# Stick-breaking attention: softplus' high parts on ScalarE, weights' sums behind the value products, head 0's scores inside the values' projection, another order at the end

## The chip, the cores and the metric

The kernel runs on one core of one Trainium2 chip. The metric is the device time of one execution in microseconds (us); of several runs the median counts.

## The reference, cut to what matters

The whole program is two transformer blocks of width 1024 over 512 tokens. The change touches one part of the second block, the stick-breaking attention with 16 heads of 64:

```python
qkv = (h @ w_qkv).reshape(b, s, 3, SB_HEADS, HEAD_DIM)
...
z = jnp.einsum('bqhd,bshd->bhqs', q_blk, k) * scale
log_1m = jnp.where(causal, jax.nn.log_sigmoid(-z), 0.0)      # minus softplus(z)
excl = lax.cumsum(log_1m, axis=3, reverse=True) - log_1m     # sum over later keys
a = jnp.where(causal, jnp.exp(jax.nn.log_sigmoid(z) + excl), 0.0)
o = jnp.einsum('bhqs,bshd->bqhd', a, v)
...
return o.reshape(b, s, SB_HEADS * HEAD_DIM) @ w_o
```

So each head needs its scores z, softplus(z), the running sum of softplus over the keys between a key and the query, the exponential of z less those sums, and the product with the values. An output projection follows over all heads.

## The kernel before, in words

Every engine works off its own queue in the order in which the code issues. There is no scheduler behind it: the order is written out by hand.

Products in full precision are built from two rounded parts of each operand, a high and a low one: three matmuls (high x high, low x high, high x low) for one. A weight matrix comes in pieces of 128 x 1024. `Weights` loads a piece by DMA on SP's queue (`ws`, L327), ScalarE rounds it to the high part (`wh`, L340), and VectorE subtracts to get the low part (`wl`, L349). `W.get` of one piece issues these two steps for the piece two further on. A projection of one piece is 24 matmuls (`group`, or `tokens` for the values).

The attention is `s_all`. Its steps:

- The values of the first eight heads are projected (`values(0)`: four weight pieces `sv0.0` to `sv0.3`, 96 matmuls into four banks of PSUM), then the norm's sums, then the projections of queries and keys of head pair 0, then the values of the other eight heads (`values(1)`). ScalarE moves the values out of PSUM. The residual is multiplied by its gain on VectorE in eight tiles (L1520, three buffers `back`) and spilled to DRAM by eight DMAs on SP's queue.
- A loop of 18 rounds follows (`for i in range(16 + last)`). In round i the table `S_ORDER` is walked: each entry names a step and its lag, so ("low", 1) in round i is the low part of head i - 1. The steps: `proj`, a projection of queries or keys of a later pair, always into the single bank `bp`; `scores` (PE, into the banks `za` and `zb`, two of each); `low` (VectorE, L1688); `evac`, the projection out of its bank (VectorE, L1611); `cap` (VectorE, two operations, L1659 and L1660); `qparts` and `kparts`, the high and low parts of queries or keys (ScalarE, VectorE, for keys two DMAs on SP's queue as well); `exp` (ScalarE, an exponential and a logarithm, L1665 and L1666); `soft`, the maximum with the scores (VectorE, L1672 and L1673); `high` (GpSimd, three operations, L1681 to L1683: a copy of 128 columns, an addition of 128 columns, the rounded copy of all 1280 columns); `weights` (PE, the sums over later keys, added to the scores in their banks: matmuls with the high parts and with the low parts of softplus); `a` (ScalarE, exponential out of the two banks, L1713 and L1714); `out` (PE, the value product, for two heads at a time in odd rounds) and `join` (ScalarE, the result out of its bank into `h`, L1733).
- While the last heads run, the output projection begins. `S_LEAD` says after which step of which round the pieces of `start(n)` are issued: products `out(m, ks)` of output tile m with the head pairs ks. `S_SPLIT` says where the pairs' results are split into high and low parts (`split(p)`: a rounded copy on ScalarE, L547, and a subtraction on VectorE, L548). Behind the loop the rest of the output projection is issued, and its results are added to the spilled residual.

Tiles with few buffers set further bounds: the high and low parts of softplus have one buffer each (`sp=1`), the capped scores two (`sT=2`).

Of the kernel before, what the change touches and what calls it, by code (L numbers as in the profile page):

```python
# [13 lines left out]
AF = mybir.ActivationFunctionType  # L14
ALU = mybir.AluOpType
# [450 lines left out]
class Kernel:  # L466
# [992 lines left out]
    def _stick(self):  # L1459
# [14 lines left out]
        for j, scale in enumerate((-NEG, 0.0, -NEG)):  # L1474
# [3 lines left out]


    S_ORDER = (("proj", 0), ("scores", 0), ("low", 1), ("evac", 0), ("cap", 0),  # L1480
               ("qparts", 0), ("kparts", 0), ("exp", 0), ("soft", 0), ("high", 0),
               ("weights", 1), ("a", 1), ("out", 2), ("join", 2))
    S_BUFS = dict(sT=2, sA=4, sp=1, st=2, back=3)
    S_LEAD = ((14, "proj"), (14, "join"), (15, "cap"), (15, "out"), (17, "kparts"))
    S_SPLIT = ((14, "cap"), (14, "scores"), (14, "out"), (14, "kparts"), (14, "out"),
               (14, "kparts"), (16, "a"))

    def s_all(self, norm, xh, xl):
        nc = self.nc
        self.turns = deque(["bp", "bo"])  # L1490

        def values(n):
            a, b, _ = self.zbanks()
            a2 = self.bank("za")
            pss = [a, a2, b[:, 0], b[:, 1]]
            for kk in range(4):
                self.tokens(pss, self.W.get(f"sv{n}.{kk}"), xh, xl, kk)
            for c, ps in enumerate(pss):
                nc.scalar.activation(self.vf[:, c, 8 * n:8 * n + 8, :],
                                     ps.rearrange("p (h d) -> p h d", h=8), AF.Copy,  # L1500
                                     scale=norm.tm[:, c:c + 1] if n else 1.0)

        values(0)
        norm.ssq()
        qk, rest = {}, []
        _, b, _ = self.zbanks(False)
        for kind in range(2):
            rest.append(self.sproj(kind, 0, xh, xl, norm, qk, b[:, kind]))
# [8 lines left out]
        for k in range(KT):  # L1517
            if isinstance(norm, Norm2):
                t = self.tmp("back", bufs=self.S_BUFS["back"])
                nc.vector.scalar_tensor_tensor(t, self.h[:, k, :], gf[:, k:k + 1],  # L1520
                                               norm.bc1, op0=ALU.mult, op1=ALU.mult)
            else:
                t = self.h[:, k, :]
            nc.sync.dma_start(out=self.dram[:, k, :], in_=t)
        self.hd, self.zs = {}, {}
        ox = None
        lead = []

        def out(m, ks):
            w, ps = lead[m]  # L1530
            self.group(ps, w, *ox, ks, 0 in ks, 7 in ks)

        def split(p):
            self.split(ox[0][:, p, :], ox[1][:, p, :], self.h[:, p, :])

        ws = []

        def start(n):

            nonlocal ox  # L1540
            if n == 0:
                ox = self.newx()
                lead.append((self.W.get("so0", 1), self.bank("bp")))
            elif n == 1:
                out(0, range(2))
            elif n == 2:
                ws.extend(self.W.get(f"so{m}", 0) for m in (1, 2))
                out(0, range(2, 6))
            elif n == 3:
                _, b, _ = self.zbanks(False)  # L1550
                for j in range(2):
                    lead.append((ws[j], b[:, j]))
                out(1, range(6))
            elif n == 4:
                ws.append(self.W.get("so3", 0))
                out(2, range(6))
                for m in range(3):
                    out(m, [6])

        last = max(lag for _, lag in self.S_ORDER)  # L1560
        self.qk, self.pend = qk, {}
        for i in range(16 + last):
            for part, lag in self.S_ORDER:
                u = i - lag
                if part == "proj":
                    if u < 14:
                        self.pend[u] = self.sproj(u % 2, u // 2 + 1, xh, xl, norm, qk)
                elif part in ("evac", "qparts", "kparts"):
                    if 0 <= u < 14 and part != ("kparts", "qparts")[u % 2]:
                        self.pend[u] = self.pend[u]()  # L1570
                elif 0 <= u < 16:
                    getattr(self, "s_" + part)(u)
                for n, (at, p) in enumerate(self.S_LEAD):
                    if (i, part) == (at, p):
                        start(n)
                for n, (at, p) in enumerate(self.S_SPLIT):
                    if (i, part) == (at, p):
                        split(n)
        split(7)
        lead.append((ws[2], self.bank("za")))  # L1580
        out(3, range(4))
        nxt, nx = self.next_norm() if self.nxt else None, self.newx() if self.nxt else None
        self.back, self.fetched, self.back_tag = {}, 0, ("back", self.S_BUFS["back"])
        self.fetch(2)
# [91 lines left out]
    def s_high(self, i):  # L1676

        t, za, zb = self.hd[i]
        s3 = self.tmp("sp3", (P, P), bufs=2)
        hi, lo = (self.tmp("sp" + a, (P, 1280), F32R, bufs=self.S_BUFS["sp"]) for a in "hl")  # L1680
        self.nc.gpsimd.tensor_scalar(s3, t[:, 1152:], 1.0, 0.0, op0=ALU.mult, op1=ALU.add)  # L1681
        self.nc.gpsimd.tensor_tensor(t[:, 1152:], t[:, 1152:], t[:, 1024:1152], op=ALU.add)
        self.nc.gpsimd.tensor_scalar(hi, t, 1.0, 0.0, op0=ALU.mult, op1=ALU.add)  # L1683
        self.hd[i] = [t, s3, hi, lo, za, zb]

    def s_low(self, i):
# [530 lines left out]
```

## Time and profile before

| | us |
|---|---|
| three runs | 2213.94, 2212.48, 2205.34 |
| median | 2212.48 |
| profiled execution | 2205.24 |
| its span | 2203.5 |

The profile is one execution, taken by the hardware profiler. Its page gives the busy time of each engine: PE is TensorE, DVE is VectorE, ACT is ScalarE, POOL is GpSimd, SP is the engine whose queue issues most DMAs. Other views list who waited for whom, the busy time in chosen stretches with the granted TensorE clock (1.00 is full), and the instructions of one engine in order of time. In these a row begins with its start, counted from the span's start, and its duration; an "x3" is three like instructions merged, and brackets hold the engine's idle time before it and what ended it. The attention lies between about 858 and 1135 us.

### The profile page before, as it was taken

The page shows a single profiled execution, that of the slowest core. Times are in us where ns is not written, and L with a number is a line of the kernel's source. Part 1 is how long each engine was busy: PE and PEld are TensorE (multiplying, and loading weights), DVE is VectorE, ACT ScalarE, POOL GpSimd, SP SyncE. Part 2 cuts the span into 40 slices and gives each one's busy share as a digit, 9 for nine tenths or more (in the row PEclk, how much of TensorE's full clock was granted, in tenths as well). Part 3 has the DMA queues.
Part 4 walks back from the last instruction along what each step waited for, and adds up shares of the span by engine and source line. Part 5 has one row for each costly group of instructions (what it writes and reads, how often), then busy time and mean ns, then how long its engine had stood idle before and what let it go on. Part 6 is the DMA issues. An engine that isn't in the chain of part 4 may idle for free.

```text
span 2203.5 us, 26617 instructions
## 1 busy us (share of the span) xinstructions
PE 2130.0 (97%) x10250; PEld 1730.3 (79%) x10250; DVE 1231.0 (56%) x2032; ACT 876.1 (40%) x1405; POOL 261.2 (12%) x324
## 2 busy tenths in 40 slices
PE   8899999999999999999999999999988899999998
PEld 6687888888888888777688888888766668888886
DVE  6988756554443435567655343446668755534334
ACT  4424434343222224355534232334547644423322
POOL 1333100000000000122200000001037730000000
PEclk9999999999999999999999999999999999999999
DMA  4222444123333323322143333334431123333331
GB/s 147 63 72 77 134 122 152 57 72 96 97 97 101 98 84 108 124 77 67 48 124 97 104 95 97 96 96 127 129 98 26 26 60 103 109 101 97 96 97 66
DMA packets 63375, 205.93 MB, mean 93 GB/s; under 512 B 7952, under 2 KB 8336, under 8 KB 63120
## 3 DMA queue, kind: packets, MB, share of 16 engines
q1 hardware_dynamic: 59504, 196.86, 30.1%
q10 hardware_dynamic: 3744, 7.37, 1.0%
q8 instruction: 80, 1.31, 0.2%
q14 instruction: 47, 0.39, 0.1%
HBM read 189.39 MB, written 6.29 MB: 89 GB/s over the span
## 4 chain that ended last, share of the span: by engine, by line
PE 78%; DVE 10%; ACT 4%; POOL 4%; issue 3%; DMA 1%; SPq 0%; ACTq 0%; POOLq 0%; DVEq 0%
PE psum L538 62%; PE b L538 14%; POOL sph L1683 1%; DVE wl L349 1%; ACT sT L1665 1%; ACT sT L1666 1%; DVE t L906 1%; PE psum L2090 1%; DVE spl L1688 1%; DVE sT L1660 1%; DVE np L2068 1%; DMA nq<-nq 1%; DVE pv L1087 0%; DVE sT L1659 0%; POOL np L2082 0%
## 5 line engine op out<-in xcount | busy, mean ns | idle before, releaser
L538 PE MATMUL psum<-xh,wh 128*128 128x512 f32 x1560 | 609.9, 391 | 1.5 <-DVE h L626 0.9
L538 PE MATMUL psum<-xh,wl 128*128 128x512 f32 x1560 | 607.5, 389 | 1.6 <-DVE wl L349 1.5
L538 PE MATMUL psum<-xl,wh 128*128 128x512 f32 x1560 | 607.2, 389 | 0.0
L340 ACT ACTIVATE wh<-ws 128x1024 fp32r<-128x1024 f32 (+1 forms) x346 | 356.5, 1039 | 371.7 <-PE psum L538 315.0
L349 DVE TENSOR_TENSOR wl<-ws,wh 128x1024 fp32r<-128x1024 f32 (+2 forms) x339 | 411.4, 1219 | 98.6 <-ACT wh L340 98.4
L538 PEld LDWEIGHTS psum<-xh,wl 128*128 128x128 f32 x1560 | 292.3, 187 | 64.8 <-DVE wl L349 2.9
L538 PEld LDWEIGHTS psum<-xh,wh 128*128 128x128 f32 x1560 | 292.4, 187 | 63.2 <-issue 2.3
L538 PEld LDWEIGHTS psum<-xl,wh 128*128 128x128 f32 x1560 | 292.4, 187 | 60.5
L538 PE MATMUL b<-xh,wh 128*128 128x512 f32 (+1 forms) x488 | 194.4, 398 | 6.6 <-ACT wh L340 6.6
L538 PE MATMUL b<-xh,wl 128*128 128x512 f32 (+1 forms) x488 | 191.9, 393 | 2.2 <-POOL wl L349 1.9
L538 PE MATMUL b<-xl,wh 128*128 128x512 f32 (+1 forms) x488 | 191.6, 393 | 0.0
L538 PE MATMUL psum<-hh,wh 128*128 128x512 f32 x320 | 125.0, 391 | 0.0
L538 PE MATMUL psum<-hh,wl 128*128 128x512 f32 x320 | 124.5, 389 | 0.0
L538 PE MATMUL psum<-hl,wh 128*128 128x512 f32 x320 | 124.5, 389 | 0.0
L1354 DVE TENSOR_TENSOR h<-h,psum 128x512 f32<-128x512 f32 x48 | 33.1, 689 | 161.2 <-PE psum L538 161.2
L1345 ACT ACTIVATE t<-t 128x512 f32<-128x512 f32 x64 | 40.5, 633 | 187.9 <-DVE t L1344 187.9
L538 PEld LDWEIGHTS b<-xh,wh 128*128 128x128 f32 (+1 forms) x488 | 92.0, 188 | 26.3 <-ACT wh L340 7.0
L538 PEld LDWEIGHTS b<-xh,wl 128*128 128x128 f32 (+1 forms) x488 | 91.5, 188 | 24.6 <-POOL wl L349 2.4
L538 PEld LDWEIGHTS b<-xl,wh 128*128 128x128 f32 (+1 forms) x488 | 92.1, 189 | 19.8 <-DVE xl L551 0.8
L1344 DVE SCALAR_TENSOR_TENSOR t<-psum,r_mlp 128x512 f32<-128x512 f32 x64 | 44.2, 690 | 79.1 <-PE psum L538 79.0
L538 PE MATMUL psum<-ks,nq 128*128 128x256 f32 (+2 forms) x256 | 72.6, 376 | 16.3 <-DVE nmx L2068 9.4
L2082 POOL TENSOR_SCALAR np<-np,nsm,gates 128x512 f32<-128x512 f32 (+3 forms) x128 | 81.8, 644 | 39.2 <-PE psum L2090 20.5
(488 smaller groups left out, 2947.1 us busy)
## 6 DMA issues: line engine op xcount, KB each, us to landing
ws<-in_wst SPq DMA_DIRECT2D x332, 512.0 KB, 3.5
h<-in_xT SPq DMA_DIRECT2D x16, 256.0 KB, 3.6
kk<-kk SPq DMA_DIRECT2D x16, 256.0 KB, 3.6
nq<-nq SPq DMA_DIRECT2D x16, 256.0 KB, 2.9
ws<-in_wst SPq DMA_DIRECT2D x8, 384.0 KB, 3.1
spill<-back SPq DMA_DIRECT2D x8, 256.0 KB, 2.0
back<-spill ACTq DMA_DIRECT2D x8, 256.0 KB, 3.6
spill<-h ACTq DMA_DIRECT2D x8, 256.0 KB, 5.7
```

The costliest lines, as they stand in the source:

```text
L340: self.nc.scalar.activation(hi[:, :n], s, AF.Copy)
L349: e.tensor_tensor(lo[:, :n], s, hi[:, :n].bitcast(F32), op=ALU.subtract)
L538: self.nc.tensor.matmul(ps, a, b, start=start, stop=stop, skip_group_check=again)
L906: nc.vector.scalar_tensor_tensor(t, u[:, q:q + T], cw[:, q:q + 1], t, op0=ALU.mult, op1=ALU.add)
L1344: nc.vector.scalar_tensor_tensor(t, ps, 0.0, norm.bc, op0=ALU.max, op1=ALU.mult)
L1345: nc.scalar.activation(t, t, AF.Square)
L1354: nc.vector.tensor_tensor(self.h[:, m, :], self.h[:, m, :], ps, op=ALU.add)
L1660: self.nc.vector.tensor_scalar(tb, zb[:, :, :384], 30.0, None, op0=ALU.min)
L1665: self.nc.scalar.activation(t, t, AF.Exp)
L1666: self.nc.scalar.activation(t, t, AF.Ln, bias=1.0)
L1683: self.nc.gpsimd.tensor_scalar(hi, t, 1.0, 0.0, op0=ALU.mult, op1=ALU.add)
L2082: self.nc.gpsimd.tensor_scalar(u["p"], u["p"], u.pop("sm"), self.gates[:, u["c"], e:e + 1], op0=ALU.mult, op1=ALU.mult)
```

## The change

Four edits in the attention:

- `s_high`: the rounded copy of softplus is divided. ScalarE copies columns 0 to 1151, GpSimd the last 128. GpSimd's other two operations stay.
- `S_ORDER`: `out` of head i - 2 is issued ahead of `weights` of head i - 1 instead of behind it, and `high` of head i behind `a` of head i - 1 instead of ahead of `weights`.
- `values(n)`: the banks are `bp`, `bo` and a `zb` pair. In `values(1)`, ahead of its third weight piece, the steps `scores`, `cap`, `exp`, `soft` and `high` of head 0 are issued; the loop leaves them out for head 0.
- The end: `S_LEAD` and `S_SPLIT` have other places. Splits begin in round 13, and their rounded copy is on GpSimd (`hi_pool=True`); the slabs that they fill are taken at the first split. Output tile 0 is issued in two parts of three pairs in round 14, tile 1 in round 15, tiles 2 and 3 in round 16; `out(3, range(4))`, which stood behind the loop and the last split, is now in round 16 ahead of the last value product.

```diff
@@ -1478,31 +1478,35 @@
 
 
     S_ORDER = (("proj", 0), ("scores", 0), ("low", 1), ("evac", 0), ("cap", 0),
-               ("qparts", 0), ("kparts", 0), ("exp", 0), ("soft", 0), ("high", 0),
-               ("weights", 1), ("a", 1), ("out", 2), ("join", 2))
+               ("qparts", 0), ("kparts", 0), ("exp", 0), ("soft", 0),
+               ("out", 2), ("weights", 1), ("a", 1), ("high", 0), ("join", 2))
     S_BUFS = dict(sT=2, sA=4, sp=1, st=2, back=3)
-    S_LEAD = ((14, "proj"), (14, "join"), (15, "cap"), (15, "out"), (17, "kparts"))
-    S_SPLIT = ((14, "cap"), (14, "scores"), (14, "out"), (14, "kparts"), (14, "out"),
-               (14, "kparts"), (16, "a"))
+    S_LEAD = ((14, "proj"), (14, "weights"), (15, "cap"), (15, "a"), (16, "out"), (16, "a"))
+    S_SPLIT = ((13, "a"), (13, "join"), (13, "join"), (14, "cap"), (14, "cap"), (14, "soft"),
+               (15, "join"))
 
     def s_all(self, norm, xh, xl):
         nc = self.nc
         self.turns = deque(["bp", "bo"])
 
         def values(n):
-            a, b, _ = self.zbanks()
-            a2 = self.bank("za")
-            pss = [a, a2, b[:, 0], b[:, 1]]
+            _, b, _ = self.zbanks(False)
+            pss = [self.bank("bp"), self.bank("bo"), b[:, 0], b[:, 1]]
             for kk in range(4):
+                if n and kk == 2:
+                    for part in ("scores", "cap", "exp", "soft", "high"):
+                        getattr(self, "s_" + part)(0)
                 self.tokens(pss, self.W.get(f"sv{n}.{kk}"), xh, xl, kk)
             for c, ps in enumerate(pss):
                 nc.scalar.activation(self.vf[:, c, 8 * n:8 * n + 8, :],
                                      ps.rearrange("p (h d) -> p h d", h=8), AF.Copy,
                                      scale=norm.tm[:, c:c + 1] if n else 1.0)
 
+        self.hd, self.zs = {}, {}
         values(0)
         norm.ssq()
         qk, rest = {}, []
+        self.qk = qk
         _, b, _ = self.zbanks(False)
         for kind in range(2):
             rest.append(self.sproj(kind, 0, xh, xl, norm, qk, b[:, kind]))
@@ -1522,7 +1526,6 @@
             else:
                 t = self.h[:, k, :]
             nc.sync.dma_start(out=self.dram[:, k, :], in_=t)
-        self.hd, self.zs = {}, {}
         ox = None
         lead = []
 
@@ -1531,21 +1534,22 @@
             self.group(ps, w, *ox, ks, 0 in ks, 7 in ks)
 
         def split(p):
-            self.split(ox[0][:, p, :], ox[1][:, p, :], self.h[:, p, :])
+            nonlocal ox
+            if p == 0:
+                ox = self.newx()
+            self.split(ox[0][:, p, :], ox[1][:, p, :], self.h[:, p, :], hi_pool=True)
 
         ws = []
 
         def start(n):
 
-            nonlocal ox
             if n == 0:
-                ox = self.newx()
                 lead.append((self.W.get("so0", 1), self.bank("bp")))
+                out(0, range(3))
             elif n == 1:
-                out(0, range(2))
+                out(0, range(3, 6))
             elif n == 2:
                 ws.extend(self.W.get(f"so{m}", 0) for m in (1, 2))
-                out(0, range(2, 6))
             elif n == 3:
                 _, b, _ = self.zbanks(False)
                 for j in range(2):
@@ -1556,9 +1560,12 @@
                 out(2, range(6))
                 for m in range(3):
                     out(m, [6])
+            elif n == 5:
+                lead.append((ws[2], self.bank("za")))
+                out(3, range(4))
 
         last = max(lag for _, lag in self.S_ORDER)
-        self.qk, self.pend = qk, {}
+        self.pend = {}
         for i in range(16 + last):
             for part, lag in self.S_ORDER:
                 u = i - lag
@@ -1568,7 +1575,7 @@
                 elif part in ("evac", "qparts", "kparts"):
                     if 0 <= u < 14 and part != ("kparts", "qparts")[u % 2]:
                         self.pend[u] = self.pend[u]()
-                elif 0 <= u < 16:
+                elif 0 <= u < 16 and (u or part not in ("scores", "cap", "exp", "soft", "high")):
                     getattr(self, "s_" + part)(u)
                 for n, (at, p) in enumerate(self.S_LEAD):
                     if (i, part) == (at, p):
@@ -1577,8 +1584,6 @@
                     if (i, part) == (at, p):
                         split(n)
         split(7)
-        lead.append((ws[2], self.bank("za")))
-        out(3, range(4))
         nxt, nx = self.next_norm() if self.nxt else None, self.newx() if self.nxt else None
         self.back, self.fetched, self.back_tag = {}, 0, ("back", self.S_BUFS["back"])
         self.fetch(2)
@@ -1680,7 +1685,8 @@
         hi, lo = (self.tmp("sp" + a, (P, 1280), F32R, bufs=self.S_BUFS["sp"]) for a in "hl")
         self.nc.gpsimd.tensor_scalar(s3, t[:, 1152:], 1.0, 0.0, op0=ALU.mult, op1=ALU.add)
         self.nc.gpsimd.tensor_tensor(t[:, 1152:], t[:, 1152:], t[:, 1024:1152], op=ALU.add)
-        self.nc.gpsimd.tensor_scalar(hi, t, 1.0, 0.0, op0=ALU.mult, op1=ALU.add)
+        self.nc.scalar.activation(hi[:, :1152], t[:, :1152], AF.Copy)
+        self.nc.gpsimd.tensor_scalar(hi[:, 1152:], t[:, 1152:], 1.0, 0.0, op0=ALU.mult, op1=ALU.add)
         self.hd[i] = [t, s3, hi, lo, za, zb]
 
     def s_low(self, i):
```

## Rows read from the trace of the kernel before

**Rows 1.** Page, part 1: busy time (share of the span), instructions of each engine

```profile
PE 2130.0 (97%) x10250; PEld 1730.3 (79%) x10250; DVE 1231.0 (56%) x2032; ACT 876.1 (40%) x1405; POOL 261.2 (12%) x324
```

**Rows 2.** Waits of PE, 880 to 1140 us: total us, times, longest

```profile
PE psum L538 <- DVE spl L1688: 7.8, 10, 1.1
PE psum L538 <- POOL sph L1683: 2.7, 2, 1.4
PE psum L538 <- DMA kk<-kk: 1.3, 1, 1.3
PE psum L538 <- ACT sA L1714: 0.6, 1, 0.6
```

**Rows 3.** Timeline, PE: start, us, operation [idle before it <- releaser]

```profile
978.36 0.44 PE L538 MATMUL psum<-spl,none 128*128 128x384 f32 x1 [0.60 <-DVE spl L1688]
...
1067.78 0.44 PE L538 MATMUL psum<-spl,none 128*128 128x384 f32 x1 [0.60 <-DVE spl L1688]
```

**Rows 4.** Windows: length, busy us per engine (x), PEclk, DMA share, GB/s

```profile
1007.00:1029.30 22.30, 21.70 (x120) 16.93 (x119) 15.60 (x18) 12.32 (x16) 5.95 (x6) 1.00 0.24 65
```

**Rows 5.** Timeline, DVE, two heads of the loop

```profile
1010.44 1.49 DVE L1688 TENSOR_TENSOR spl<-sT,sph 128x1280 fp32r<-128x1280 f32 x1 [1.16 <-POOL sph L1683]
...
1021.52 1.49 DVE L1688 TENSOR_TENSOR spl<-sT,sph 128x1280 fp32r<-128x1280 f32 x1 [1.16 <-POOL sph L1683]
...
1028.39 0.95 DVE L1673 TENSOR_TENSOR sT<-sT,psum 128x768 f32<-128x768 f32 x1
1030.41 1.22 DVE L349 TENSOR_TENSOR wl<-ws,wh 128x1024 fp32r<-128x1024 f32 x1 [1.07 <-ACT wh L340]
1032.79 1.49 DVE L1688 TENSOR_TENSOR spl<-sT,sph 128x1280 fp32r<-128x1280 f32 x1 [1.16 <-POOL sph L1683]
```

**Rows 6.** Timeline, POOL, high parts: first head, then a head of the loop

```profile
931.08 1.26 POOL L1683 TENSOR_SCALAR sph<-sT 128x1280 fp32r<-128x1280 f32 x1
...
1030.45 2.30 POOL L1683 TENSOR_SCALAR sph<-sT 128x1280 fp32r<-128x1280 f32 x1
```

**Rows 7.** Timeline, ACT, the second of these heads

```profile
1026.48 1.27 ACT L1666 ACTIVATE sT<-sT 128x1280 f32<-128x1280 f32 x1
...
1028.82 0.60 ACT L1733 ACTIVATE h<-psum 128x512 f32<-128x512 f32 x1
1029.30 1.07 ACT L340 ACTIVATE wh<-ws 128x1024 fp32r<-128x1024 f32 x1
```

**Rows 8.** Timeline, PE: first matmuls of projection, scores, next projection

```profile
916.70 0.39 PE L538 MATMUL psum<-xh,wh 128*128 128x512 f32 x1
...
922.14 0.39 PE L538 MATMUL psum<-sq,kk 128*128 128x512 f32 x1
...
923.79 0.45 PE L538 MATMUL psum<-xh,wh 128*128 128x512 f32 x1
```

**Rows 9.** Timeline, DVE, from the values' projection to the first head

```profile
909.49 2.07 DVE L1520 SCALAR_TENSOR_TENSOR back<-h,cols,r_end 128x512 f32<-128x512 f32 x3
...
918.58 1.22 DVE L349 TENSOR_TENSOR wl<-ws,wh 128x1024 fp32r<-128x1024 f32 x1
922.34 0.69 DVE L1611 SCALAR_TENSOR_TENSOR st<-psum,r_begin 128x512 f32<-128x512 f32 x1 [2.54 <-PE psum L538]
...
928.21 0.95 DVE L1673 TENSOR_TENSOR sT<-sT,psum 128x768 f32<-128x768 f32 x1
```

**Rows 10.** Timeline, ACT and DVE, the last join and the last split

```profile
1109.61 0.60 ACT L1733 ACTIVATE h<-psum 128x512 f32<-128x512 f32 x1 [6.18 <-PE psum L538]
...
1110.90 0.69 DVE L548 TENSOR_TENSOR xl<-h,xh 128x512 fp32r<-128x512 f32 x1 [6.21 <-ACT xh L547]
```

**Rows 11.** Timeline, PE, an idle stretch early in the kernel

```profile
70.52 0.69 PE L538 MATMUL b<-adt,small 128*128 128x64 f32 x2 [4.29 <-DVE adt L987]
```

**Rows 12.** Windows, as rows 4, after idle stretches of PE

```profile
72.00:74.00 2.00, 2.00 (x9) 1.25 (x8) 2.00 (x5) 1.22 (x2) 0.00 (x0) 0.50 0.18 74
...
1080.00:1082.00 2.00, 2.00 (x9) 1.81 (x8) 1.81 (x4) 1.87 (x2) 0.00 (x0) 0.50 0.04 8
```

## Prediction

> **What bounds the kernel now.** I read the page's busy shares first: TensorE is busy for 2130.0 of 2203.5 us [rows 1], so an edit elsewhere counts only through the time in which TensorE stands still. Next, who TensorE waits for in the stretch that the change touches: 7.8 us for the low parts of softplus (`spl`), 2.7 for the high parts (`sph`), 1.3 for the keys' DMA and 0.6 for the weights' exponential, together 12.4 us [rows 2]. By place: the ten waits for `spl` are four of 1.1, five of 0.60 and one of 0.5, the two for `sph` 1.3 and 1.4. Three of 1.1 and the 1.3 fall on the first three heads (4.5 us); the five of 0.60 on the loop, one per two heads, first at 978.36 and last at 1067.78 [rows 3]; the rest on the last heads (4.8 us). A perfect change is therefore worth these 12.4 us and the half-clock stretch described below, some 14 us or 0.65%. Last, the loop's engines in order of time. Over two heads PE works 21.70 of 22.30 us [rows 4], and the low parts start at 1010.44, 1021.52 and 1032.79, 11.08 and 11.27 us apart [rows 5]. No row in that round waits for PE: low parts, evacuation, cap, exponential, logarithm, maximum, POOL's high parts, next low parts. So VectorE, ScalarE and GpSimd set the round's 22.35 us and PE is 0.6 us short of it.
>
> **Loop: the high parts on ScalarE, the sums behind the value products.** From the start of a low part to the end of the maximum it takes 1028.39 + 0.95 - 1021.52 = 7.82 us [rows 5], and nothing of that changes. Before, the next low part followed 3.45 us later (11.27 - 7.82; 3.26 for the other head), waiting for POOL. Its copy takes 2.30 us there and 1.26 where VectorE is idle [rows 6]. Now ScalarE copies 1152 of 1280 columns: between 1.07 (1024 columns) and 1.27 (1280) [rows 7]; I take 1.17 by columns. POOL keeps small operations: the two ahead of its copy end 1.1 us after the maximum (1030.45 - 1029.34) and a 128-column copy follows; they hide beside ScalarE's.
>
> What ScalarE's queue does with it decides. The next weight piece's high part (`wh`, L340) stood right behind the exponential, and its low part (`wl`, L349) ran on VectorE while POOL copied. Now `wh` stands behind the new copy, which waits for the maximum, and `wl` stands ahead of the low parts on VectorE. So from the maximum's end: 0.09 to start, 1.07 for the copy less its overlap, 0.48 for the join (1028.82 to 1029.30, every second head), 1.11 to the start of `wl` (1029.30 to 1030.41) [rows 5, 7], and 1.14 for `wl` (1.22 less overlap): 3.89 us with a join, 3.41 without, instead of 3.45 and 3.26. The round becomes 22.35 + 0.44 + 0.15 = 22.94 us. POOL's 2.3 us are saved, and the weights' split that hid beside them is what is late next. The sums behind the value products do fill PE's old wait, but a longer round only moves it: 22.94 - 21.70 = 1.24 us per round instead of 0.60. Five rounds: **+3.2 us**, and 1.3 more or less for the copy's bounds over 13 heads.
>
> **Start: scores of head 0 inside the values' projection.** PE's work is only moved: 1.65 us (922.14 to 923.79), between products of 5.44 us per 24 matmuls (916.70 to 922.14) [rows 8]. But all that the head issues moves too. Its scores start two weight pieces before 916.70, at 905.8. Before, the maximum ended 928.21 + 0.95 - 922.14 = 7.0 us after that point [rows 8, 9]; here, at 912.8. Behind it in program order stand, on ScalarE, the high copy (1.17) and two `wh`, on VectorE two `wl`: 912.8 + 0.1 + 1.1 + 1.1 + 1.2 + 1.2 = 917.5. Only then VectorE reaches the eight products for the residual that is spilled (L1520), which ran from 909.49 [rows 9]: 8 us later. With their waits for their own DMAs and the `wl` behind them they ended at 918.58 + 1.22 = 919.8, so now at 927.8; behind them in VectorE's queue stands the evacuation of the first projection in the loop (0.69 [rows 9]), and the second projection needs that evacuation, since `bp` is one bank. PE has ended the first at 916.70 + 1.65 + 5.44 = 923.8, has no scores left to put between, and starts the second at 928.5: 4.7 us idle. The three early waits go, 0.6 us of one comes back at head 1: 5.3 against 4.5, **+0.8 us**. SP's spills and the loads queued behind them slide by the same 8 us; loads are three pieces ahead, so I price that at 0 to 2 us and take 0. The values' new banks are shared with the norm's sums; the first two are closed 9 and 6 matmuls ahead of the end, so 0 to 0.7, taken 0.
>
> **End: output products and splits earlier, splits' high parts on GpSimd.** L is the start of low part 12. PE's 21.70 less two projections and two scores [rows 4, 8] leaves 7.5 us for a value product and two heads' sums, 2.5 each. PE ends the sums of head 12 near L + 4.3. Next stand three output products, ahead of the last pair's scores, and their low part waits behind maximum 13: L + 7.82 + 0.69 (a split's VectorE part [rows 10]) = L + 8.5. Less the one matmul that needs no low part: 3.9 us idle. Splits 1 and 2 queue on POOL behind head 13's three operations: POOL copies of 512 columns at 0.55 (1.26 us x 512/1280 and start-up) make the last one ready at L + 11.2, 1.0 more idle. So the scores, and with them the whole chain of head 14, start later than the loop would let them. The sixth split stands behind maximum 14 (scores at L + 11.9, 7.0 to the maximum, 0.7), while PE runs out of work at L + 17.4: 2.2. Output 1 needs the bank that exponential 14 frees, now with no value product between it and the sums: 1.25 instead of 0.60. And out(3), which covered the last join and split (1109.61 to 1111.59 [rows 10]), has gone ahead of the last value product: join, copy and subtraction stand bare, 2.0. Sum 10.35 against 1.27 + 1.40 + 1.08 + 0.49 + 0.60 = 4.84: **+5.5 us**.
>
> GpSimd's copies here depend on what VectorE does beside them: 2.30 against 1.26 us [rows 6]. The Trainium skill, SBUF — State Buffer, "SBUF: two separate sides", says that a VectorE operation with two SBUF inputs and a GpSimd operation that reads SBUF take a shared port pair in turn, the later one blocked for a whole instruction. The added 1.04 us agrees with one `wl` (1.22); by the rule splits 1 and 2 would each lose up to a subtraction more, and the sum would be about 1 us higher.
>
> **Clock.** After PE stood 4.29 us its clock was at 0.50 in 72 to 74 us, 1.2 of 2.4 GHz [rows 11, 12]; after the end's waits, at 0.50 in 1080 to 1082 [rows 12] (by the lengths of the matmuls around them for some 3.6 us, a loss of 1.8). I keep one such stretch at the end, as now. The Trainium skill, TensorE: Matmul & The Clock Gate, "Part 1: The HAM clock gate", says that the low level is the default which activity lifts; by it the new idle place at the start would be followed by half clock as well, which is the second rival.
>
> **Sum.** 0.8 + 3.2 + 5.5 = +9.5 us, 0.43%: 2214.7 against the profiled execution's 2205.24 (span 2203.5). That execution is at the fast edge of the three runs, 7.2 us below their median of 2212.48; on the median the forecast is 2222.0.
>
> **Rivals.**
> (1) It is faster: the loop fits under PE's 21.70 us, and the early scores and splits close the ends. For it: PE lacks only 0.6 us a round. Price: a third to all of the 14 us, -5 to -14, 2198 to 2208. It decides by the distance from maximum to low part: it must be under 21.70/2 - 7.82 = 3.0 us, while `wh` and `wl` alone take 2.25 behind a 1.16 copy. Chance 0.14, half of it above 0.5%.
> (2) Half clock after the start's 4.7 us and once more at the end: 1.8 each, as now at the end: about +13, 2225.6. For: 4.7 us is longer than the 4.29 that half clock followed [rows 11, 12]; against: one case, early in the kernel and after other work. It decides from the start's gap alone: with the evacuation ahead of L1520's waits there is none. Chance 0.27.
> (3) ScalarE's copy and GpSimd's addition write and read parts of the same tiles; were it held until the addition ends, each head costs about 1 us more: +13 on top, 2235. Chance 0.06.
> (4) It does nothing that can be seen: waits move, +-4, 2209 to 2216. Chance 0.08.
> (5) The forecast, +5 to +12: 0.45.
>
> **Range and chances.** From rival 1's milder half to rival 2 with its unknowns: 2207 to 2232. The measurement tells 0.5% (11 us) from no change. Faster: half of (1), 0.07. Slower: (2), (3) and a tenth of (5), 0.38. Same: 0.55.
>
> **What would show it.** Right: PE idle some 4.7 us ahead of the second projection, with L1520 late; low parts 11.2 and 11.7 us apart with `wl` right ahead of them; PE waiting for `xl` around the last scores and before the last output product. Wrong: low parts under 11 us apart, `wl` early, or PE busy without a break through the start. If the maximum-to-low distance comes out as written and the time falls, the error lies in the ends.

## The result, and the profile after

| | before | after |
|---|---|---|
| median of ten runs, us | 2209.37 | 2222.25 |
| lowest, highest | 2204.95, 2213.94 | 2217.17, 2227.77 |
| profiled execution | 2205.24 | 2217.73 |
| its span | 2203.5 | 2215.9 |

The ratio after to before is 1.0056, 95% interval 1.0043 to 1.0069: the changed kernel is slower by about 0.6%, with the 0.5% that a measurement tells from no change inside the interval. The medians are 12.9 us apart and the spans of the two profiled executions 12.4, so these show nearly all of the difference.

The page of after, part 1 (columns as [rows 1]), and who PE waited for from 880 to 1150 us (total us, times, longest):

```profile
PE 2133.9 (96%) x10250; PEld 1731.3 (78%) x10250; DVE 1228.2 (55%) x2032; ACT 889.8 (40%) x1413; POOL 239.9 (11%) x332
...
PE psum L538 <- DVE st L1616: 5.9, 1, 5.9
PE psum L538 <- DVE xl L548: 5.8, 4, 3.4
PE psum L538 <- DVE spl L1694: 5.8, 6, 1.1
PE psum L538 <- POOL xh L545: 1.8, 2, 1.4
PE psum L538 <- ACT sA L1720: 0.9, 1, 0.9
```

PE does the same 10250 matmuls, and the work did move from GpSimd to ScalarE (POOL 261.2 to 239.9 us, ACT 876.1 to 889.8). PE's waits grew from 12.4 us [rows 2] to 20.2. The waits for `sph` are gone, as the edit says; in their place stand the first evacuation `st`, the splits' `xl` and `xh`, and still `spl`. By place: start 6.4 us (4.5 before), loop five waits of 1.07 (five of 0.60, [rows 3]), end 8.5 (4.8).

**Start.** Timeline of VectorE and of PE in after (start, us, operation, idle before it), then windows with columns as [rows 4]:

```profile
915.61 2.36 DVE L349 TENSOR_TENSOR wl<-ws,wh 128x1024 fp32r<-128x1024 f32 x2 [2.24 <-ACT wh L340]
917.89 2.07 DVE L1524 SCALAR_TENSOR_TENSOR back<-h,cols,r_end 128x512 f32<-128x512 f32 x3
924.42 2.08 DVE L1524 SCALAR_TENSOR_TENSOR back<-h,cols,r_end 128x512 f32<-128x512 f32 x3 [4.46 <-DMA spill<-back]
927.30 1.41 DVE L1524 SCALAR_TENSOR_TENSOR back<-h,cols,r_end 128x512 f32<-128x512 f32 x2 [0.80 <-DMA spill<-back]
928.63 1.22 DVE L349 TENSOR_TENSOR wl<-ws,wh 128x1024 fp32r<-128x1024 f32 x1
929.77 0.68 DVE L1616 SCALAR_TENSOR_TENSOR st<-psum,r_begin 128x512 f32<-128x512 f32 x1
...
930.51 0.80 PE L538 MATMUL psum<-xh,wh 128*128 128x512 f32 x1 [5.94 <-DVE st L1616]
...
924.00:932.00 8.00, 2.06 (x7) 1.36 (x6) 6.05 (x9) 1.47 (x3) 0.00 (x0) 0.76 0.59 210
932.00:940.00 8.00, 8.00 (x34) 6.25 (x33) 4.47 (x6) 1.75 (x3) 0.00 (x0) 0.82 0.29 99
```

The residual's products begin at 917.89 instead of 909.49 [rows 9]. Three buffers let three of them go, the fourth waits 4.46 us for the spill of the first, and the evacuation at 929.77 waits behind them all. PE stands 5.94 us, and the matmul that it starts with takes 0.80 us where one at full clock took 0.39 [rows 8]: the clock had fallen, by 24% in the mean of these 8 us, in most of which PE stood idle, and by 18% in the next 8, in which it worked throughout.

**Loop.** Timelines of VectorE and ScalarE over a round of two heads, and GpSimd's addition:

```profile
1012.08 0.95 DVE L1678 TENSOR_TENSOR sT<-sT,psum 128x768 f32<-128x768 f32 x1
1015.78 1.22 DVE L349 TENSOR_TENSOR wl<-ws,wh 128x1024 fp32r<-128x1024 f32 x1 [2.75 <-ACT wh L340]
1016.92 1.48 DVE L1694 TENSOR_TENSOR spl<-sT,sph 128x1280 fp32r<-128x1280 f32 x1
...
1023.72 0.94 DVE L1678 TENSOR_TENSOR sT<-sT,psum 128x768 f32<-128x768 f32 x1
1026.92 1.23 DVE L349 TENSOR_TENSOR wl<-ws,wh 128x1024 fp32r<-128x1024 f32 x1 [2.26 <-ACT wh L340]
1028.07 1.48 DVE L1694 TENSOR_TENSOR spl<-sT,sph 128x1280 fp32r<-128x1280 f32 x1
...
1013.14 1.17 ACT L1688 ACTIVATE sph<-sT 128x1152 fp32r<-128x1152 f32 x1 [0.52 <-DVE sT L1678]
1014.22 0.58 ACT L1739 ACTIVATE h<-psum 128x512 f32<-128x512 f32 x1
1014.69 1.05 ACT L340 ACTIVATE wh<-ws 128x1024 fp32r<-128x1024 f32 x1
...
1013.59 0.46 POOL L1687 TENSOR_TENSOR sT<-sT 128x128 f32<-128x128 f32 x1
```

Between the maximum's end and the low part stand, one behind the other, the copy of 1.17, the join, `wh` and `wl`: 3.89 us with a join (1013.03 to 1016.92), 3.41 without (1024.66 to 1028.07). Before, the `wl` at 1030.41 ran beside the copy on GpSimd [rows 5, 6].

**End.** PE's waits in order of time, GpSimd's copies, VectorE beside them, and a window:

```profile
1082.04 0.79 PE L538 MATMUL psum<-xl,wh 128*128 128x512 f32 x1 [3.39 <-DVE xl L548]
1083.71 0.80 PE L538 MATMUL psum<-xh,wh 128*128 128x512 f32 x1 [0.45 <-POOL xh L545]
...
1095.45 0.50 PE L538 MATMUL psum<-xl,wh 128*128 128x512 f32 x1 [1.86 <-DVE xl L548]
...
1122.84 0.51 PE L538 MATMUL psum<-xh,wh 128*128 128x512 f32 x1 [1.40 <-POOL xh L545]
...
1071.78 0.62 POOL L545 TENSOR_SCALAR xh<-h 128x512 fp32r<-128x512 f32 x1
...
1084.20 1.05 POOL L545 TENSOR_SCALAR xh<-h 128x512 fp32r<-128x512 f32 x1
...
1086.23 1.85 POOL L545 TENSOR_SCALAR xh<-h 128x512 fp32r<-128x512 f32 x1
...
1081.30 0.68 DVE L548 TENSOR_TENSOR xl<-h,xh 128x512 fp32r<-128x512 f32 x1
1083.68 1.08 DVE L548 TENSOR_TENSOR xl<-h,xh 128x512 fp32r<-128x512 f32 x1 [1.70 <-POOL xh L545]
...
1085.71 1.89 DVE L1694 TENSOR_TENSOR spl<-sT,sph 128x1280 fp32r<-128x1280 f32 x1
...
1070.00:1096.00 26.00, 19.98 (x97) 13.97 (x96) 17.28 (x21) 13.58 (x16) 8.99 (x14) 0.87 0.15 41
```

The output products wait for the low part of a split that stands behind maximum 13; a split's copy takes 0.62 us alone, 1.05 beside a subtraction (1084.20) and 1.85 beside a low part (1086.23), and VectorE beside a copy takes 1.08 for a subtraction that took 0.68 just before; the window has the clock at 0.87 in the mean, so 0.13 x 26 = 3.4 us are lost to half clock besides.

**The sum.** For all kernels below I take one stretch, called the attention: from the start of the first evacuation of the values to the start of the last of the eight residual additions. It is split into PE's waits, the clock's loss (the part of full speed not granted, times the length, over its windows), and the rest. What lies ahead of it and behind it is left out: the first evacuation starts between 878.2 and 884.1 us in the kernels of this study, though no edit touches the work before it; some 1.4 of the 12.4 us between the two profiled executions lie ahead of it and behind it, most of them behind it, and stay unexplained.

| | attention | PE waits | clock's loss | rest |
|---|---|---|---|---|
| before | 263.1 | 12.4 | 1.7 | 249.0 |
| after | 274.1 | 20.2 | 6.8 | 247.1 |

The attention is 11.0 us longer: 7.8 of waits, 5.1 of clock, less 1.9 of rest. But the two middle columns overlap where PE stands idle at half clock. The stretch of the wait of 5.94 us in after:

```profile
924.57:930.51 5.94, 0.00 (x1) 0.01 (x1) 5.08 (x7) 0.03 (x1) 0.00 (x0) 0.80 0.58 223
```

PE does nothing in it, and 0.20 x 5.94 = 1.2 us of the clock's loss are counted in it a second time; with the waits of the end it is 1.7 us, and in before none. So the clock cost 3.4 us and not 5.1 on top of the waits (2.2 at the start, and 2.9 instead of 1.7 at the end), and the rest is nearly equal, 248.8 and 249.0. The tables keep the plain loss.

### The profile page after: what moved, and what is told of

Its sections match the earlier page's. It is cut to its first block, busy times and chain, and to the rows that moved or that the text cites. A ratio compares the mean times of both kernels' runs of the same rounds, so it can differ in the third digit from the quotient of the medians.

```text
span 2215.9 us, 26619 instructions
## 1 busy us (share of the span) xinstructions
PE 2133.9 (96%) x10250; PEld 1731.3 (78%) x10250; DVE 1228.2 (55%) x2032; ACT 889.8 (40%) x1413; POOL 239.9 (11%) x332
## 4 chain that ended last, share of the span: by engine, by line
PE 45%; DVE 2%; issue 1%; POOL 1%; ACT 1%; DMA 1%; ACTq 0%; DVEq 0%; POOLq 0%; SPq 0%
PE psum L538 44%; PE psum L2096 1%; DVE np L2074 1%; DMA nq<-nq 1%; POOL np L2088 0%; DVE wl L349 0%; POOL np L2181 0%; PE psum L401 0%; DVE xl L551 0%; DMA wd_causal<-in_wide 0%; DVE t L1344 0%; ACT t L1345 0%; PE psum L1380 0%; DVE xl L548 0%; PE psum L434 0%
## 6 DMA issues: line engine op xcount, KB each, us to landing
h<-in_xT SPq DMA_DIRECT2D x16, 256.0 KB, 3.9
kk<-kk SPq DMA_DIRECT2D x16, 256.0 KB, 3.4
nq<-nq SPq DMA_DIRECT2D x16, 256.0 KB, 2.9
spill<-back SPq DMA_DIRECT2D x8, 256.0 KB, 2.0
back<-spill ACTq DMA_DIRECT2D x8, 256.0 KB, 3.4
spill<-h ACTq DMA_DIRECT2D x8, 256.0 KB, 5.6
```

## The experiments

Theories. **Q**: the edits' order in the queues costs the time; `wl` and the residual's products stand ahead of what PE needs next. **C**: the copy on ScalarE costs it by itself. **H**: half clock behind the new waits is the main loss, also in the runs' spread. Three kernels undo one part each, one makes one part alone, the others move what Q accuses. A table behind them has all times.

**u_start**: the early scores undone.

```diff
-            pss = [self.bank("bp"), self.bank("bo"), b[:, 0], b[:, 1]]
+            pss = [a, a2, b[:, 0], b[:, 1]]
             for kk in range(4):
-                if n and kk == 2:
-                    for part in ("scores", "cap", "exp", "soft", "high"):
-                        getattr(self, "s_" + part)(0)
...
-                elif 0 <= u < 16 and (u or part not in ("scores", "cap", "exp", "soft", "high")):
+                elif 0 <= u < 16:
```

> The changed kernel with its start undone: head 0's scores and softplus are back in the loop, the values in their old banks. Loop and end stay changed. Theory Q (queues: work was put behind other work on engines that work in order): L1524's products run beside the values' projection again, the 5.9 us gap of PE ahead of the second projection goes, and waits of about 1 us return for heads 0 to 2, 3 to 4.5 us together; with the half clock behind the gap (some 2 us) the time falls 3 to 5 us below the changed kernel, and low parts stay 11.2 and 11.6 us apart. Theory C (ScalarE's copy itself is what costs): the time stays within 2 us. Theory H (the half clock behind the long gap is the main loss): it falls by 5 us or more, and the spread of 9 us between runs of the changed kernel goes.

The attention fell by 2.45 us, less than the 3 to 5 expected of the time, whose ratio fell by 0.0016 or 3.5 us. The 5.94 us gap is gone, but the first head's low part now comes late behind `wl` (one wait of 2.7), and of the clock's loss 1.7 went at the start (1.7 instead of 3.4) and came back at the end (5.1 instead of 3.4). The waits by releaser, the line that changed:

```profile
PE psum L538 <- DVE spl L1692: 8.1, 6, 2.7
```

**u_copy**: the whole rounded copy on GpSimd again.

```diff
-        self.nc.scalar.activation(hi[:, :1152], t[:, :1152], AF.Copy)
-        self.nc.gpsimd.tensor_scalar(hi[:, 1152:], t[:, 1152:], 1.0, 0.0, op0=ALU.mult, op1=ALU.add)
+        self.nc.gpsimd.tensor_scalar(hi, t, 1.0, 0.0, op0=ALU.mult, op1=ALU.add)
```

> The changed kernel with the copy undone: GpSimd rounds all 1280 columns again; order, start and end stay changed. Q: wh and wl no longer stand behind the copy; low parts 11.1 and 11.3 us apart again, PE's waits in the loop 0.6 instead of 1.07 us, the gap at the start 1 to 2 us shorter; time 3 to 6 us lower than the changed kernel. C: the same direction and size, so this run gives the size of the part and does not tell Q from C. H: a gap of over 4 us stays, so the time falls by 3 us at most.

A miss: 1.25 us less. The loop did go back (low parts 11.08 and 11.26 us apart, waits of 0.63) and the start's gap shrank to 3.71, so PE waits 3.1 us less; but the clock lost 6.8 us at the end instead of 3.4. The new order of `S_ORDER` is still in this kernel, and its loop is that of before (0.60, 11.08 and 11.27), so in the loop the order alone is worth nothing that shows; no kernel undoes it by itself.

**u_end**: the old `S_LEAD` (its fourth entry one step later), `S_SPLIT`, `start` and splits on ScalarE, `out(3, range(4))` behind the loop again.

```diff
-    S_LEAD = ((14, "proj"), (14, "weights"), (15, "cap"), (15, "a"), (16, "out"), (16, "a"))
-    S_SPLIT = ((13, "a"), (13, "join"), (13, "join"), (14, "cap"), (14, "cap"), (14, "soft"),
-               (15, "join"))
+    S_LEAD = ((14, "proj"), (14, "join"), (15, "cap"), (15, "a"), (17, "kparts"))
+    S_SPLIT = ((14, "cap"), (14, "scores"), (14, "out"), (14, "kparts"), (14, "out"),
+               (14, "kparts"), (16, "a"))
...
-            self.split(ox[0][:, p, :], ox[1][:, p, :], self.h[:, p, :], hi_pool=True)
+            self.split(ox[0][:, p, :], ox[1][:, p, :], self.h[:, p, :])
...
```

> The changed kernel with the end undone: old places of the products and splits of the output projection (the product of tile 1 one step later, since its bank is freed one step later now), splits' high parts on ScalarE, out(3) behind the loop. Start and loop stay changed. Q: the waits for xl and xh at the end (3.4, 0.5, 0.3, two for the sixth split, two for the last, 7.6 us together) go, waits for the keys' DMA and for head 13's low parts return (2 to 4 us); the half clock at the end stays at most once; time 3 to 6 us below the changed kernel. C: no change over 2 us.

3.5 us less, in the expected range; the clock's loss is the same as in after. The refilled end was a loss, though its old form waits as well, now longest 2.8 us for the keys' DMA. By PE's waits each of the three parts undone so far gives back 3.0 to 3.2 us; what sets the three attentions apart is mostly the clock.

**d_high**: the kernel before with only the divided copy (the two new lines of `s_high`, at the step's old place in the order).

```diff
-        self.nc.gpsimd.tensor_scalar(hi, t, 1.0, 0.0, op0=ALU.mult, op1=ALU.add)
+        self.nc.scalar.activation(hi[:, :1152], t[:, :1152], AF.Copy)
+        self.nc.gpsimd.tensor_scalar(hi[:, 1152:], t[:, 1152:], 1.0, 0.0, op0=ALU.mult, op1=ALU.add)
```

> The kernel before with the copy alone: ScalarE rounds 1152 columns, at the old place ahead of the weights' sums and of the exponential; no other edit. Q: on ScalarE the exponential of the head before, the join and wh all stand behind the copy, and wl and the next low parts behind wh; from maximum to low part 4.6 us without and 5.1 us with a join instead of 3.26 and 3.45, the round 25.3 instead of 22.35 us, attention some 15 to 20 us longer than 263.1. C (the copy's own duration is what costs, 1.2 against GpSimd's 2.1 to 2.3): the round gets shorter or stays.

As Q had it in the loop: the round is 12.34 + 12.82 = 25.16 us. The attention is 23.0 us longer than before, above the 15 to 20 expected. ScalarE and VectorE in a round:

```profile
1018.17 1.17 ACT L1683 ACTIVATE sph<-sT 128x1152 fp32r<-128x1152 f32 x1 [1.70 <-DVE sT L1673]
1019.24 0.58 ACT L1714 ACTIVATE sA<-psum 128x512 f32<-128x512 f32 x1
1019.72 0.81 ACT L1715 ACTIVATE sA<-psum 128x768 f32<-128x768 f32 x1
1020.41 0.60 ACT L1734 ACTIVATE h<-psum 128x512 f32<-128x512 f32 x1
1020.89 1.07 ACT L340 ACTIVATE wh<-ws 128x1024 fp32r<-128x1024 f32 x1
...
1021.99 1.22 DVE L349 TENSOR_TENSOR wl<-ws,wh 128x1024 fp32r<-128x1024 f32 x1 [3.93 <-ACT wh L340]
1023.13 1.48 DVE L1689 TENSOR_TENSOR spl<-sT,sph 128x1280 fp32r<-128x1280 f32 x1
```

The high parts are ready at 1019.34, but the low part starts at 1023.13, because VectorE stands at `wl`, which waits for a `wh` that stands behind two exponentials and a join. The change's new order takes the exponentials out from between; it leaves `wl` where it is.

**wl_late**: after, with the loop's `wl` issued behind the low part (behind the step `kparts`) instead of by `W.get`.

```diff
-    def get(self, name, look=LOOK):
+    def get(self, name, look=LOOK, low=True):
...
-        self.make(i + look)
+        self.hi(i + look)
+        if low:
+            self.lo()
...
+                if part == "kparts":
+                    self.W.lo()
...
-        self.group(ps, self.W.get(("sq", "sk")[kind] + str(p)), xh, xl, range(KT), True, True)
+        self.group(ps, self.W.get(("sq", "sk")[kind] + str(p), low=p == 0), xh, xl, range(KT), True, True)
```

> The changed kernel with one thing moved: in the loop the subtraction for the weights' low part (wl, L349) is issued behind the keys' or queries' parts, where VectorE waits for the exponential, instead of ahead of the low parts of softplus. The copy stays on ScalarE. Q: maximum to low part falls from 3.4 and 3.85 us to about 1.3, the round from 22.8 to PE's own 21.7, PE's five waits of 1.07 us vanish; PE then idles nowhere between 950 and 1070; time 5 to 7 us below the changed kernel. C: the copy still sets the round, low parts stay over 11 us apart, time within 2 us of the changed kernel.

A miss on the good side: 11.9 us less. A window of the whole loop, VectorE around a low part, and PE's waits from 880 to 1150 us:

```profile
940.00:1070.00 130.00, 130.00 (x714) 103.49 (x714) 94.65 (x111) 89.22 (x103) 13.65 (x37) 1.00 0.27 76
...
1009.72 0.95 DVE L1682 TENSOR_TENSOR sT<-sT,psum 128x768 f32<-128x768 f32 x1
1012.30 1.49 DVE L1698 TENSOR_TENSOR spl<-sT,sph 128x1280 fp32r<-128x1280 f32 x1 [1.63 <-ACT sph L1692]
...
PE psum L540 <- DVE st L1620: 4.7, 1, 4.7
PE psum L540 <- DVE xl L550: 3.5, 4, 1.9
PE psum L540 <- POOL xh L547: 2.3, 2, 1.4
PE psum L540 <- ACT sA L1724: 0.9, 1, 0.9
```

The low part waits for the copy itself, 1.63 us, instead of 3.4 to 3.9 behind `wl`. PE works through all of the loop's 130.00 us (124.23 in after), and two heads take 9.68 + 11.77 = 21.45 us: PE bounds the round. The end gains too: the wait for the first split's low part, behind the maximum, falls from 3.39 to 0.78 us, while the two waits behind it grow, from 0.45 and 0.32 to 0.95 and 0.62. C falls: the copy stayed on ScalarE.

**back_late**: after, with the residual's products taken out of the start and issued behind `kparts` of rounds 0 to 3, three, two, two and one.

```diff
-        for k in range(KT):
+        def residual(k):
...
+                if part == "kparts":
+                    for k in ((0, 1, 2), (3, 4), (5, 6), (7,))[i] if i < 4 else ():
+                        residual(k)
```

> The changed kernel with one thing moved: the eight products for the spilled residual (L1524) and their DMAs are issued in rounds 0 to 3 of the loop, three, two, two and one of them, behind the keys' or queries' parts, instead of all eight ahead of the loop. Q: the first projection's evacuation is no longer behind them; PE's gap ahead of the second projection falls from 5.9 us to under 1, and the half clock behind it goes; the attention (from the first evacuation of the values to the last residual addition: 263.1 us before, 274.1 with the change) gets 5 to 7 us shorter. The loop's waits of 1.07 stay. H: the same, and more than the gap's 5 us goes. C: no effect on the gap's end beyond what the copy sets, under 2 us.

3.4 us less, below the range. At the start all went as expected; the gain was given back at the end:

```profile
925.83 0.50 PE L538 MATMUL psum<-xh,wh 128*128 128x512 f32 x1 [0.78 <-DVE st L1620]
...
924.00:932.00 8.00, 7.22 (x32) 5.48 (x31) 6.19 (x8) 2.32 (x3) 0.00 (x0) 1.00 0.42 156
1070.00:1096.00 26.00, 19.95 (x90) 13.62 (x89) 17.48 (x21) 13.59 (x16) 7.71 (x11) 0.80 0.09 26
```

The gap is 0.78 instead of 5.94 and the clock stays at 1.00, so the residual's products made both losses of the start but for this 0.78. In the last window PE is as busy as in after (19.95 against 19.98), yet the clock's mean is 0.80 instead of 0.87: 1.8 us more lost there, and 3.4 more (6.8 against 3.4) in all of the end. Why as long waits brought more half clock, no run here shows.

**both_late**: after, with the edits of wl_late and of back_late, as shown above, together.

> back_late and wl_late together in the changed kernel. Q: the two parts are at different places and add: from wl_late's attention of 262.2 us another 4 to 7 us, 255 to 258, so 5 to 8 us under the kernel before. If PE was bound elsewhere by then (a rival: the early heads' softplus comes late for other reasons), under 2 us more than wl_late.

260.2 us, 2 above the range: the waits fell to 7.6, but the clock lost 5.1 at the end.

**all_three**: both, and the end mended: the first splits issued ahead of the steps that delayed them, and `out(3, range(4))` behind the last split, so that it covers it again.

```diff
-    S_LEAD = ((14, "proj"), (14, "weights"), (15, "cap"), (15, "a"), (16, "out"), (16, "a"))
-    S_SPLIT = ((13, "a"), (13, "join"), (13, "join"), (14, "cap"), (14, "cap"), (14, "soft"),
+    S_LEAD = ((14, "proj"), (14, "weights"), (15, "cap"), (15, "a"), (16, "out"))
+    S_SPLIT = ((13, "kparts"), (13, "soft"), (13, "soft"), (14, "cap"), (14, "cap"), (14, "cap"),
                (15, "join"))
...
         split(7)
+        lead.append((ws[2], self.bank("za")))
+        out(3, range(4))
```

> both_late with the end in another order: the first split behind the keys' parts of round 13 and the next two behind its maximum, the sixth ahead of maximum 14, and out(3, range(4)) behind the loop and the last split again. Q: the waits for xl and xh at the end (0.8, 1.0, 0.6, 1.9, 1.4, 0.2 in wl_late) shrink to under 3 us together; attention 252 to 256 us, the kernel 0.3 to 0.5% faster than before. Rival: a(14)'s wait of 0.9 grows by as much as the others shrink, since PE reaches it earlier; then within 1 us of both_late.

253.0 us, in the range; all of PE's waits in the attention are these:

```profile
PE psum L540 <- ACT sA L1727: 2.4, 1, 2.4
PE psum L540 <- DVE st L1623: 0.9, 1, 0.9
PE psum L540 <- DVE xl L550: 0.5, 1, 0.5
```

It beats both kernels: 0.9952 of before (0.9937 to 0.9967).

**three_pool**: all_three with the diff of u_copy, to see what the copy on ScalarE is worth when `wl` is out of the way.

> all_three with GpSimd rounding all 1280 columns again. Q: once wl stands behind the keys' or queries' parts, either engine's copy is off PE's path, so moving it to ScalarE is worth nothing: attention within 1.5 us of all_three's 253.0, no waits of PE in the loop; wl no longer runs beside GpSimd's copy, which takes about 1.3 us. Rival (ScalarE's copy is what lets the round fit): PE waits in the loop return, 0.4 us or more a round, attention over 255.

A miss: 256.3 instead of within 1.5 of 253.0. PE waits four times, 2.6 us in all, for `spl` again: at the first heads (947.8 and 969.9) and the last (1077.0 and 1086.6). In the loop Q held: the round is 10.23 + 11.22 = 21.45 us, PE's own, with either copy. So the copy on ScalarE is worth about 3 us at the two ends of the attention once `wl` doesn't stand behind it, by one profile each; the intervals of the whole times overlap.

**b_wl_late**: the diff of wl_late alone, on the kernel before.

> The kernel before with wl moved alone: behind the keys' or queries' parts instead of ahead of the low parts; GpSimd still copies all 1280 columns. Two theories of the gain of wl_late. Q: in the kernel before wl was hidden beside GpSimd's copy, so what changes is that the copy runs without VectorE beside it: 1.3 us instead of 2.1 to 2.3, low parts 10.1 to 10.4 us apart by themselves, PE's waits of 0.6 and 1.1 us in the loop vanish, attention 3 to 6 us shorter than 263.1. Rival (the order alone helps only where ScalarE copies): GpSimd's copy stays over 2 us and the attention within 1 us of 263.1.

A miss on the good side: 7.1 us less than before. GpSimd's copy and VectorE in a round:

```profile
1008.33 1.26 POOL L1687 TENSOR_SCALAR sph<-sT 128x1280 fp32r<-128x1280 f32 x1
...
1009.62 1.49 DVE L1692 TENSOR_TENSOR spl<-sT,sph 128x1280 fp32r<-128x1280 f32 x1 [2.41 <-POOL sph L1687]
```

Here too the subtraction was moved and nothing else. GpSimd's copy takes 1.26 us in the loop instead of 2.30 [rows 6], and the low part starts as it ends.

**after_b**: the changed kernel once more, with no edit, for the spread.

> The changed kernel unchanged, another execution with a profile, for the spread of 2217 to 2228 us between its runs. H: the idle places in the attention are the same (20.2 us), but the half clock behind them differs between executions, and a run of over 2225 us lies 3 us or more above the 6.8 us lost to the clock in the attention. Rival: the attention takes 274 +- 1 us again, and the spread comes from stretches ahead of it or behind it (the first evacuation of the values then lies later than 878.7 us).

Its span is 2221.6, 5.7 us above after's. 3.6 of that lie ahead of the attention (first evacuation at 882.3 instead of 878.7), 2.5 inside it, most of that the clock at the end (5.1 instead of 3.4). PE's waits agree, 20.5 and 20.2. So the start's gap isn't what spreads the runs, and H falls in that point: u_start's five runs do lie within 2.9 us, but back_late, without the gap, runs from 2211.0 to 2223.0. Two attentions of one kernel can thus differ by 2.5 us, most of it clock, so 2.45 and 1.25 in u_start and u_copy are no more than that by themselves.

| | attention | PE waits | clock's loss | median, us | ratio to before (95%) |
|---|---|---|---|---|---|
| before | 263.1 | 12.4 | 1.7 | 2209.37 | 1 |
| after | 274.1 | 20.2 | 6.8 | 2222.25 | 1.0056 (1.0043 to 1.0069) |
| u_start | 271.7 | 17.1 | 6.8 | 2215.12 | 1.0040 (1.0025 to 1.0054) |
| u_copy | 272.9 | 17.1 | 8.5 | 2218.75 | 1.0049 (1.0032 to 1.0066) |
| u_end | 270.6 | 17.3 | 6.8 | 2215.31 | 1.0037 (1.0023 to 1.0051) |
| d_high | 286.1 | 25.6 | 10.3 | 2232.38 (one run) | |
| wl_late | 262.2 | 11.4 | 3.4 | 2210.37 | 1.0017 (1.0004 to 1.0030) |
| back_late | 270.7 | 15.6 | 6.8 | 2218.43 | 1.0036 (1.0021 to 1.0050) |
| both_late | 260.2 | 7.6 | 5.1 | 2204.80 | 0.9979 (0.9965 to 0.9994) |
| all_three | 253.0 | 3.8 | 1.7 | 2199.34 | 0.9952 (0.9937 to 0.9967) |
| three_pool | 256.3 | 7.9 | 0 | 2202.63 | 0.9968 (0.9954 to 0.9983) |
| b_wl_late | 256.0 | 7.0 | 1.7 | 2199.36 | 0.9957 (0.9943 to 0.9972) |
| after_b | 276.6 | 20.5 | 8.5 | 2223.44 (one run) | |

Each ratio is to runs of before that were taken beside that kernel's, with medians of 2208.1 to 2211.8, so it is not the quotient of two medians of this table. The rest, attention less waits and clock, is 246.5 to 250.2 in all. The attention tells all_three and b_wl_late 3 us apart; the times of whole executions do not.

## Why the prediction was right or wrong

The forecast, 2222.0 us, came out (2222.25), and the sign and the mechanism with it, but closer than its working deserves. It stood on a median of 2212.48 for before, and ten runs gave 2209.37, so the step to be explained was 12.9 us, not 9.5: a base 3.1 too high and a step 3.4 too small cancelled, which is luck; and of its four terms two were too small and two too big. In the attention 9.5 us were forecast and 11.0 found.

- **Loop, +3.2; found +2.35.** The mechanism is shown: 3.89 and 3.41 us from maximum to low part, to the hundredth, the copy at 1.17, wl right ahead of the low part; d_high made it worse and wl_late took it away. The term was too big by a little: the low parts are 11.15 and 11.63 us apart (11.23 and 11.71 forecast), as the 7.82 from low part to maximum shrank to 7.74, so the round is 22.78 and PE waits 1.07 instead of 1.24. PE's own work for two heads, 21.70 in the forecast, is 21.45 in wl_late, where nothing holds it up.
- **Start, +0.8; found +1.9.** The chain is the forecast's: products begin at 917.9 (917.5 forecast), the evacuation stands behind them, head 1 waits 0.42 (0.6). But the gap is 5.94 us instead of 4.7. The step that was off is "with their waits for their own DMAs", which I took over with the old times: the fourth product waited 4.46 us for the first spill. back_late, where 0.78 us of the gap are left, shows that the products made the rest of it.
- **End, +5.5; found +3.7.** Of the single terms 3.9 was 3.39, 1.0 was 0.45 + 0.32, 2.2 was 1.86, 1.25 was 0.90, 2.0 was 1.40 + 0.22. All five places are there, each smaller. The splits' copies at 0.55 were 0.62 alone, 1.05 beside a subtraction and 1.85 beside a low part. The Trainium skill, SBUF — State Buffer, "SBUF: two separate sides", says that such a copy and such a subtraction take turns. The trace agrees with it where they met: the copy of 1086.23 ended 0.48 us after the low part that ended at 1087.60. But the copies of splits 1 and 2 started ahead of the subtractions and took 0.62 us each, so the extra microsecond that was priced for them did not come.
- **Clock, 0; found +5.1, of which 3.4 on top of the waits.** This is the step that failed. I kept one half-clock stretch at the end and made the second rival, "half clock after start's 4.7 us and once more at the end", worth 0.27. It came in: 3.4 us at the start, 3.4 at the end instead of 1.7 (2.2 and 2.9 without what lies under the waits). The terms of start and clock were too small by 4.5 us; against them stand the loop and the end, too big by 2.7, and a rest 0.2 lower. The Trainium skill, TensorE: Matmul & The Clock Gate, "Part 1: The HAM clock gate", makes the low level the default. The start agrees with it: from 924 to 932 us the clock was at 0.76 in after, where PE stood 5.94 us, and at 1.00 in back_late, where it stood 0.78.
- **Rivals.** The first (faster) needed less than 3.0 us from maximum to low part with `wl` and `wh` behind the copy; that was right as a condition, and wl_late meets it by taking `wl` away. The third (the copy held by GpSimd's addition) is refuted: the copy starts 0.11 us after the maximum ends (1013.03 to 1013.14) and runs to 1014.31, beside GpSimd's addition (1013.59 to 1014.05). The chances leaned to "same"; the ratio lies at 0.56%, and its interval on both sides of 0.5%.
- **Not settled:** how much half clock a wait at the end brings. The attention's end lost 0 to 6.8 us to it, and the waits do not order the kernels: the same seven waits at the end, 6.7 us together, went with 1.7 in wl_late and with 5.1 in both_late, and the changed kernel itself lost 3.4 there in after and 5.1 in after_b.

## What to carry to other kernels

An operation taken off a slow engine is worth only what the queue behind it lets through: list what stands between its end and its consumer on every engine, prefetch work too. Here one subtraction that prepares a later weight, issued with the prefetch instead of behind the critical step, cost 7 to 12 us of the attention, more than any of the three edits that were undone one at a time gave back (1.25 to 3.5). When a step is moved earlier, look at everything that it pushes back, above all operations that wait for their own DMAs, and price an idle place together with the clock that follows it.

## What the runs showed of the hardware that was not expected

- GpSimd's rounded copy and VectorE's subtraction of two tiles did not share, they took turns: the one that started later ended its own time, less some 0.14 us, after the other's end. The copy of 1280 columns takes 1.26 us in the loop when `wl` does not run beside it and 2.30 when it does, and then it ends 1.12 us after the `wl` [rows 5, 6], which keeps its 1.22. Which engine pays goes by who starts first: VectorE's low part at 1085.71 started while the copy of 1085.22 ran and took 1.89 us, 1.48 in the loop.
- The same waits at the end were followed by different clocks: 0.87 and 0.80 in the mean over 1070 to 1096 us in after and back_late, with PE busy for 19.98 and 19.95 us.
